# A decoder block on one core: low parts of one weight sum made by VectorE, output quarters of the down projection finished later, adaLN sums moved

## The chip, the cores and the metric

The kernel runs on one core of a Trainium2 chip. The metric is the device time of one execution in microseconds (us), the median of several. The engines are TensorE (PE, matmuls; PEld is its weight load), VectorE (DVE), ScalarE (ACT), GpSimd (POOL) and SyncE (SP, which here only issues DMAs). Each engine runs its own instructions in order and waits on semaphores for the others.

## The reference

One layer of a decoder block on x (512 tokens of 1024 channels, fp32), with a conditioning vector c. What matters here:

```python
mod = silu(c) @ ada_w + ada_b            # 6 x 1024: shift1, scale1, gate1, shift2, scale2, gate2
h   = rms_norm(x, norm1_g) * (1 + scale1) + shift1
...                                       # input projection, block-sparse attention, pooling, gates -> merged
x   = x + gate1 * (merged @ w_out)                       # "out"
h2  = rms_norm(x, norm2_g) * (1 + scale2) + shift2
u   = causal_dwconv3(h2 @ w_up) ; u_g, u_v = split(u)    # "up", 2 x 2816 channels
x   = x + gate2 * ((silu(u_g) * u_v) @ w_down)           # "down"
```

## The kernel before, in words

**Precision.** Each fp32 operand is split in two: a high part (a copy rounded to the type float32r) and a low part (the operand minus its high part). A product is three matmuls: high·high, low·high, high·low. They stand in helpers, so the profile names them by L133 to L135 and L139 to L141. The high copy is made by ACT (L114, L219), the low part by DVE (L124, L220).

**Products of blocks.** out, most of up, and down are computed as 2x2 blocks with seven products instead of eight. The seven are a11·b11, a12·b21, s1·t1, s2·t2, s4·b22, s3·t3, a22·t4: s are sums of blocks of the activations, t sums of blocks of the weights. In out, PE goes through them in that order (`o_prod`); in down the list `phases` (loop variable n, from 0) has the order a11·b11, s1·t1, s2·t2, a12·b21, s3·t3, s4·b22, a22·t4. The accumulators are PSUM banks called X, Y and Z, one for each of two row tiles p. A bank is copied or read between products (`o_keep`, `o_add`; `keep`, `finish`) and then accumulated further.

**Weights.** A unit is a tile of 128 x 1024. `load_unit` (L82) loads it on the SP queue to one of five buffers ("raw") that are used in rotation: a load waits until the tile five loads earlier has been read. Sums of weights (tsum for down, osum for out) are made in DRAM by accumulating DMAs on POOL's queue, long before they are used.

**out.** `o_split` loads a unit and has ACT make the two high parts and DVE the two low parts. The weight sum t3, fifth of the seven weight forms in the kernel's list FORMS, goes another way: `o_high` has ACT make the high parts and then negate the raw tile in place (L1043); POOL issues four DMAs that add the high parts to the negated tile (L1045); later `o_low` has ACT copy these, negated again, as the low parts (L1052). In ACT's order `o_low` stands behind the high parts of t4 and ahead of the squares of rows' tiles 0 and 1 (L1018), which the second RMS norm needs. That norm goes on with a sum on DVE (ms_y, L1022), a power on POOL (rs_y, L1024) and a scaling on DVE (xn, L1029). Behind s3·t3 and six matmuls of a22·t4, PE transposes the normalised tiles (`turn_h2(1)`, L907, tiles hT), then does the rest of a22·t4 and the first halves of up's units 0 and 1, then the second transposes (`turn_h2(3)`). `take_h2` turns them into h2 on ACT and DVE. POOL's queue in this stretch also holds the stores of x to DRAM (x2d, L1032) and fetches of x (L987).

**adaLN sums.** mod is 48 sums of 128 x 1024 on DVE (`ada_col(g, k)`: a load on SP and L207). Those of gate2, `ada_col(5, k)`, are spread: k = 0 in up's unit 3, k = 1 to 3 at the end of up, the rest in down.

**up.** Loop over 22 units j: matmuls on PE; two units behind them the convolution on ACT and DVE (`behind(0)`, L1127, L1131) and the gated product (`behind(1)`, L1146, L1153). Weights of unit j + 1 are prepared during unit j. The sums of down's weights run on POOL's queue at the same time.

**down.** For each of the seven products six units i; `unit` prepares the weights two units ahead. When a quarter of the output is complete, `finish` does three DVE steps of 128 x 512 (L1405 to L1413) and an output DMA on SP (L1414) for each of two row tiles.

The engines PE, DVE and ACT run in the order in which the code emits their instructions (`manual_schedule`); POOL and SP are ordered by the framework's scheduler.

Of the kernel before, what the change touches and what calls it, by code (L numbers as in the profile page):

```python
# [55 lines left out]
def block_kernel(tc, x, cvec, ada, wtok, wch, pool_w, wbr, wout, wup, wdn, pack, table, out):  # L56
# [4 lines left out]
    with ctx:  # L61
# [18 lines left out]
        def load_unit(src, name):  # L80
            raw = wraw_p.tile([P, src.shape[-1]], F32, tag="raw", name=f"raw_{name}")
            nc.sync.dma_start(raw, src)  # L82
            return raw
# [127 lines left out]
        def ada_col(g, k):  # L211
            ada_sum(g, k, ada_load(g, k))
# [820 lines left out]

        def o_high(nm):

            res = []
            for i in range(2):
                raw = load_unit(osrc(nm, i), f"wo_{nm}_{i}")
                for s in range(2):
                    hi = slot(f"wo_{nm}_{2 * i + s}_h", F32R)  # L1040
                    nc.scalar.activation(hi, raw[:, s * 512 : s * 512 + 512], AF.Copy)
                    res.append((hi, raw[:, s * 512 : s * 512 + 512]))
                nc.scalar.activation(raw, raw, AF.Copy, scale=-1.0)  # L1043
            for hi, r in res:
                nc.gpsimd.dma_start(r, hi.bitcast(F32), accum_op=ALU.add)  # L1045
            return res

        def o_low(nm, res):

            for k, (hi, r) in enumerate(res):  # L1050
                lo = slot(f"wo_{nm}_{k}_l", F32R)
                nc.scalar.activation(lo, r, AF.Copy, scale=-1.0)  # L1052
                wo[nm, k] = hi, lo

        o_prod("a11", "b11", "X", by_k=True)
# [23 lines left out]
        g_lo("s3")  # L1079
        t3 = o_high("t3")  # L1080
        for p in range(2):
# [4 lines left out]
        for i in range(2):  # L1086
            o_split("t4", i)
        o_low("t3", t3)
        o_prod("s4", "b22", "Y")
# [228 lines left out]
        for i in range(4):  # L1318
            ahead(f"up{i}", min(2, 2 * PLAIN - 1 - i))
            first.append((ready.pop(f"up{i}"), bank(f"u_{i}")))  # L1320
            up_mm(first[i][1], first[i][0], 0, 256)
            if i == 1:
                take_h2(3, turn_h2(3))
        for w, ps in first:
            up_mm(ps, w, 256, 512)
# [16 lines left out]
        for j in range(NP):  # L1342
# [18 lines left out]
            else:  # L1361
# [12 lines left out]
                if j in (2, 3):  # L1374
                    h_forms(j)
                if j == 3:
                    ada_col(5, 0)
            pend.append((j, *u))
# [4 lines left out]
        s_forms(NU - 2)  # L1383
        for k in range(1, 4):
            ada_col(5, k)
# [48 lines left out]
        def split_s(i):  # L1434
            forms["s2", i] = split_act(fa["s2", i], f"s2_{i}", width(i) // 2)

        for n, (an, bn, acc) in enumerate(phases):
            last = n == len(phases) - 1
            held_ = []
            for i in range(NU):  # L1440
                if n == 0 and i == 0:
                    ahead("b11_0", 3)
                w = unit(f"{bn}_{i}")
                a = forms.pop((an, i))
                if last and i >= NU - 2:
# [32 lines left out]
            if n == 0:  # L1478
                keep("s1", "X")
            elif n == 1:  # L1480
                keep("s5", "Y")
                g2 = row_of(5, "g2")
            elif n == 2:
                keep("s2", "X")
                fetch(0, 0)
            elif n == 3:
                for p in range(2):
                    finish(p, 0, 0, "Z", plus="s1")
                fetch(1, 1)
            elif n == 4:  # L1490
                for p in range(2):
                    finish(p, 1, 1, "X", minus=("s5", None))
                fetch(0, 1)
            elif n == 5:
                for p in range(2):
                    finish(p, 0, 1, "Y", minus=(None, "s2"))
                fetch(1, 0)
# [69 lines left out]
```

## Time and profile before

| | us |
|---|---|
| median of 3 runs | 668.15 |
| lowest, highest | 667.65, 668.96 |
| the profiled execution | 668.46 |
| its span in the trace | 666.7 |
| mean granted clock of PE | 0.992 |

Of one execution the profile has every instruction with start and duration, and what an idle engine waited for. A timeline row reads: start, duration, engine, line, operation, output<-input, size, xcount of merged instructions, and in brackets the idle time before it and who ended it. A windows row reads: stretch, length, then for PE, PEld, DVE, ACT and POOL the busy time with the number of instructions, then PE's granted clock, the DMA share and GB/s. Buffer numbers in names are left out there, so wo_t is any of the sums t1 to t4 of out. The end of a matmul is modelled, and neighbours overlap; the pace is seen in the starts.

### The profile page before, as it was taken

Reading aid. Unit: us, or ns where it says so; the run is one execution under the profiler, and the core shown is the slowest. Engines: PE = TensorE matmul, PEld = TensorE weight load, DVE = VectorE, ACT = ScalarE, POOL = GpSimd, SP = SyncE. Lnnn points to the kernel's source line nnn. Section 1 sums busy time; section 2 is a strip of 40 time slices with the busy share of each in tenths; the row PEclk is TensorE's granted clock in tenths of the full one; section 3 lists DMA queues with packets and bytes.
Section 4 is the critical chain, followed back from the end, with each engine's and each line's share of the span. In section 5 each row is a group of like instructions: output and inputs, shape, how many; then the busy total and the mean of one; then the engine's idle time right before and its main releaser. Section 6 shows DMA issues by size and latency. Waiting matters only on the chain.

```text
span 666.7 us, 9758 instructions
## 1 busy us (share of the span) xinstructions
PE 653.1 (98%) x3469; PEld 560.2 (84%) x3469; DVE 564.1 (85%) x966; ACT 392.3 (59%) x687; POOL 180.7 (27%) x243
## 2 busy tenths in 40 slices
PE   8999999999999999997999999999999999999997
PEld 6788788888888888875998899998999987888786
DVE  6997887898878868984869899998999799998775
ACT  8564346757655547583855575665756654758331
POOL 3004064432100055532544444444431000010000
PEclk9999999999999999996999999999999999999999
DMA  8887359999842785576489999999997235868761
GB/s 349 321 305 257 97 176 243 271 316 257 281 160 96 252 183 204 183 227 215 133 253 236 290 273 287 277 256 272 263 279 212 100 126 166 268 181 310 264 216 63
DMA packets 49031, 151.99 MB, mean 228 GB/s; under 512 B 6499, under 2 KB 7180, under 8 KB 48982
## 3 DMA queue, kind: packets, MB, share of 16 engines
q1 hardware_dynamic: 29510, 101.38, 44.7%
q0 software_dynamic: 19472, 49.98, 29.1%
q8 instruction: 27, 0.44, 0.3%
q14 instruction: 22, 0.18, 0.1%
HBM read 130.34 MB, written 19.95 MB: 225 GB/s over the span
## 4 chain that ended last, share of the span: by engine, by line
PE 81%; DVE 7%; DMA 5%; ACT 4%; issue 2%; POOL 1%; SPq 0%; ACTq 0%; DVEq 0%; POOLq 0%
PE u L134 6%; PE u L135 6%; PE u L133 6%; PE gate_ps L133 4%; PE gate_ps L135 4%; PE gate_ps L134 4%; PE uX L139 3%; PE uX L141 3%; PE uX L140 3%; DMA raw_wo_t<-wo_t_h 2%; PE q L149 2%; PE p L149 2%; PE X L140 2%; DMA raw_b<-in_wdn 2%; PE X L141 2%
## 5 line engine op out<-in xcount | busy, mean ns | idle before, releaser
L134 PE MATMUL u<-h2l,hi_up 128*128 128x512 f32 (+1 forms) x224 | 80.5, 360 | 0.1
L133 PE MATMUL u<-h2h,hi_up 128*128 128x512 f32 (+1 forms) x224 | 80.5, 359 | 0.0
L135 PE MATMUL u<-h2h,lo_up 128*128 128x512 f32 (+1 forms) x224 | 80.3, 359 | 0.0
L207 DVE CUSTOM_DVE_ANT_0 raw_ada<-raw_ada,cbc,pk 128x1024 f32<-128x1024 f32 x48 | 60.7, 1277 | 0.1
L133 PE MATMUL gate_ps<-h_h,hi_gate 128*128 128x512 f32 x128 | 50.1, 391 | 0.0
L135 PE MATMUL gate_ps<-h_h,lo_gate 128*128 128x512 f32 x128 | 50.0, 390 | 0.0
L134 PE MATMUL gate_ps<-h_l,hi_gate 128*128 128x512 f32 x128 | 49.9, 390 | 0.0
L134 PEld LDWEIGHTS u<-h2l,hi_up 128*128 128x128 f32 x224 | 42.3, 189 | 6.4 <-DVE h2l L923 0.3
L135 PEld LDWEIGHTS u<-h2h,lo_up 128*128 128x128 f32 x224 | 42.3, 189 | 6.2
L133 PEld LDWEIGHTS u<-h2h,hi_up 128*128 128x128 f32 x224 | 42.3, 189 | 6.1
L766 POOL DMA_DIRECT2D ta<-in_wdn x33 | 30.3, 917 | 19.1 <-DMA tsum_t<-ta 6.4
L841 POOL DMA_DIRECT2D g_d<-acol x2 | 1.8, 922 | 120.6 <-DVE acol L207 120.6
L767 POOL DMA_DIRECT2D tsum_t<-ta x33 | 18.6, 564 | 55.4 <-DMA ta<-in_wdn 52.2
L114 ACT ACTIVATE hi_t<-raw_t 128x1024 fp32r<-128x1024 f32 (+1 forms) x24 | 23.6, 985 | 16.8 <-PE X L141 7.1
L124 DVE TENSOR_TENSOR lo_t<-raw_t,hi_t 128x1024 fp32r<-128x1024 f32 (+1 forms) x24 | 26.6, 1129 | 4.2 <-ACT hi_t L114 4.2
L607 ACT ACTIVATE L<-L,mn 128x512 f32<-128x512 f32 (+3 forms) x32 | 17.6, 552 | 19.9 <-DVE mn L603 19.9
L135 PEld LDWEIGHTS gate_ps<-h_h,lo_gate 128*128 128x128 f32 x128 | 24.0, 188 | 5.1
L133 PEld LDWEIGHTS gate_ps<-h_h,hi_gate 128*128 128x128 f32 x128 | 24.0, 188 | 4.9 <-DVE mn L603 0.3
L134 PEld LDWEIGHTS gate_ps<-h_l,hi_gate 128*128 128x128 f32 x128 | 24.0, 188 | 4.5
L114 ACT ACTIVATE hi_up<-raw_up 128x1024 fp32r<-128x1024 f32 x24 | 24.9, 1049 | 4.3 <-PE u L134 4.3
L114 ACT ACTIVATE hi_b<-raw_b 128x1024 fp32r<-128x1024 f32 (+1 forms) x18 | 17.5, 983 | 16.3 <-PE X L141 4.9
L124 DVE TENSOR_TENSOR lo_b<-raw_b,hi_b 128x1024 fp32r<-128x1024 f32 (+1 forms) x18 | 19.9, 1129 | 6.0 <-ACT hi_b L114 6.0
(417 smaller groups left out, 2201.3 us busy)
## 6 DMA issues: line engine op xcount, KB each, us to landing
raw_ada<-in_ada SPq DMA_DIRECT2D x48, 512.0 KB, 5.5
raw_up<-in_wup SPq DMA_DIRECT2D x44, 512.0 KB, 6.5
ta<-in_wdn POOLq DMA_DIRECT2D x44, 256.0 KB, 6.4
raw_t<-tsum_t SPq DMA_DIRECT2D x20, 512.0 KB, 4.6
tsum_t<-ta POOLq DMA_DIRECT2D x33, 256.0 KB, 4.9
raw_gate<-in_wch SPq DMA_DIRECT2D x16, 512.0 KB, 4.4
raw_b<-in_wdn SPq DMA_DIRECT2D x15, 512.0 KB, 5.7
tc<-in_wdn POOLq DMA_DIRECT2D x22, 256.0 KB, 5.7
```

The lines of the kernel that those rows point to most:

```text
L114: nc.scalar.activation(hi, raw, AF.Copy)
L124: nc.vector.tensor_sub(lo, raw, hi.bitcast(F32))
L133: nc.tensor.matmul(ps, sh, mh, start=start, stop=False)
L134: nc.tensor.matmul(ps, sh, ml, start=False, stop=False)
L135: nc.tensor.matmul(ps, sl, mh, start=False, stop=stop)
L139: nc.tensor.matmul(ps, sh, mh, start=start, stop=False, skip_group_check=True)
L140: nc.tensor.matmul(ps, sh, ml, start=False, stop=False, skip_group_check=True)
L141: nc.tensor.matmul(ps, sl, mh, start=False, stop=stop, skip_group_check=True)
L149: nc.tensor.matmul(ps, sl if i else sh, mh if i else ml, start=False, stop=stop and i != late)
L207: nc.vector.tensor_tensor_reduce(out=raw, in0=raw, in1=cbc, op0=ALU.mult, op1=ALU.add, scale=1.0, scalar=col(C_AB + i), accum_out=acol[:, ...
L766: add = lambda to, nm: nc.gpsimd.dma_start(to, src(nm, i)[:, us], accum_op=ALU.add)
L767: store = lambda nm, t: nc.gpsimd.dma_start(dst[nm, i][:, us], t)
```

## The change

Three edits. (1) t3 of out goes through `o_split` like the others: its low parts are made by DVE, ahead of those of t4, and the functions `o_high` and `o_low` are gone. (2) `ada_col(5, 0)` and `ada_col(5, 1)` move from up's unit 3 and from the end of up to the place right behind the second transposes' `take_h2`. (3) In down, the `finish` of the three quarters that complete with n = 3, 4 and 5 is no longer done at the end of that product but, one row tile each, behind the weight preparation of units 0 and 1 of the next product.

```diff
-        def o_high(nm):
-            res = []
-            for i in range(2):
-                raw = load_unit(osrc(nm, i), f"wo_{nm}_{i}")
-                for s in range(2):
-                    hi = slot(f"wo_{nm}_{2 * i + s}_h", F32R)
-                    nc.scalar.activation(hi, raw[:, s * 512 : s * 512 + 512], AF.Copy)
-                    res.append((hi, raw[:, s * 512 : s * 512 + 512]))
-                nc.scalar.activation(raw, raw, AF.Copy, scale=-1.0)
-            for hi, r in res:
-                nc.gpsimd.dma_start(r, hi.bitcast(F32), accum_op=ALU.add)
-            return res
-        def o_low(nm, res):
-            for k, (hi, r) in enumerate(res):
-                lo = slot(f"wo_{nm}_{k}_l", F32R)
-                nc.scalar.activation(lo, r, AF.Copy, scale=-1.0)
-                wo[nm, k] = hi, lo
...
-        t3 = o_high("t3")
+        for i in range(2):
+            o_split("t3", i)
...
-        o_low("t3", t3)
...
                 take_h2(3, turn_h2(3))
+                ada_col(5, 0)
+                ada_col(5, 1)
...
-                if j == 3:
-                    ada_col(5, 0)
...
-        for k in range(1, 4):
+        for k in range(2, 4):
             ada_col(5, k)
...
+        due = []
...
                 w = unit(f"{bn}_{i}")
+                if due:
+                    due.pop(0)()
...
             elif n == 3:
-                for p in range(2):
-                    finish(p, 0, 0, "Z", plus="s1")
+                due = [lambda p=p: finish(p, 0, 0, "Z", plus="s1") for p in range(2)]
                 fetch(1, 1)
```

n == 4 and n == 5 are changed as n == 3 is.

ACT in out, before: from the copies of product s2·t2 (ok_s2) to the squares of tiles 0 and 1 (junk_y); _h and _l are high and low parts.

```order
L981 ACTIVATE ok_s2_0_3200<-oX_0_2961 128x512
L981 ACTIVATE ok_s2_1_3202<-oX_1_2965 128x512
L219 ACTIVATE wo_t4_0_h_3210<-raw_wo_t4_0_3208 128x512
L219 ACTIVATE wo_t4_1_h_3214<-raw_wo_t4_0_3208 128x512
L219 ACTIVATE wo_t4_2_h_3220<-raw_wo_t4_1_3218 128x512
L219 ACTIVATE wo_t4_3_h_3224<-raw_wo_t4_1_3218 128x512
L1052 ACTIVATE wo_t3_0_l_3228<-raw_wo_t3_0_3152 128x512
L1052 ACTIVATE wo_t3_1_l_3230<-raw_wo_t3_0_3152 128x512
L1052 ACTIVATE wo_t3_2_l_3232<-raw_wo_t3_1_3159 128x512
L1052 ACTIVATE wo_t3_3_l_3234<-raw_wo_t3_1_3159 128x512
L1018 ACTIVATE junk_y0_1_3264,ss_y0_3170<-x2_0_1_3124 128x512
L1018 ACTIVATE junk_y1_1_3270,ss_y1_3173<-x2_1_1_3126 128x512
```

The same place after:

```order
L981 ACTIVATE ok_s2_0_3202<-oX_0_2961 128x512
L981 ACTIVATE ok_s2_1_3204<-oX_1_2965 128x512
L219 ACTIVATE wo_t4_0_h_3212<-raw_wo_t4_0_3210 128x512
L219 ACTIVATE wo_t4_1_h_3216<-raw_wo_t4_0_3210 128x512
L219 ACTIVATE wo_t4_2_h_3222<-raw_wo_t4_1_3220 128x512
L219 ACTIVATE wo_t4_3_h_3226<-raw_wo_t4_1_3220 128x512
L1018 ACTIVATE junk_y0_1_3258,ss_y0_3172<-x2_0_1_3124 128x512
L1018 ACTIVATE junk_y1_1_3264,ss_y1_3175<-x2_1_1_3126 128x512
```

The four low parts of t3 have left ACT's order; they stand on DVE ahead of the four of t4.

DVE in down, before: the low parts of weight units (lo_t3_1 is unit 1 of t3) around the first `finish` (dt) and the last low parts of activations.

```order
L124 TENSOR_TENSOR lo_t3_1_6688<-raw_t3_1_6684,hi_t3_1_6686 128x1024
L220 TENSOR_TENSOR s4_5_l_6697<-s1_5_6178,s4_5_h_6696 128x256
L220 TENSOR_TENSOR a22_5_l_6701<-a22_5_6116,a22_5_h_6700 128x256
L1405 TENSOR_TENSOR dt_0_0_0_6704<-Z_0_6122,s1_0_6257 128x512
L1412 TENSOR_TENSOR dt_0_0_0_6704<-dt_0_0_0_6704,g2_0_6410 128x512
L1413 TENSOR_TENSOR dt_0_0_0_6704<-dt_0_0_0_6704,x2r_0_0_6550 128x512
L1405 TENSOR_TENSOR dt_1_0_0_6709<-Z_1_6123,s1_1_6259 128x512
L1412 TENSOR_TENSOR dt_1_0_0_6709<-dt_1_0_0_6709,g2_0_6410 128x512
L1413 TENSOR_TENSOR dt_1_0_0_6709<-dt_1_0_0_6709,x2r_1_0_6552 128x512
L124 TENSOR_TENSOR lo_t3_2_6722<-raw_t3_2_6718,hi_t3_2_6720 128x1024
L124 TENSOR_TENSOR lo_t3_3_6740<-raw_t3_3_6736,hi_t3_3_6738 128x1024
```

The same place after:

```order
L124 TENSOR_TENSOR lo_t3_2_6706<-raw_t3_2_6702,hi_t3_2_6704 128x1024
L1384 TENSOR_TENSOR dt_0_0_0_6708<-Z_0_6116,s1_0_6251 128x512
L1391 TENSOR_TENSOR dt_0_0_0_6708<-dt_0_0_0_6708,g2_0_6404 128x512
L1392 TENSOR_TENSOR dt_0_0_0_6708<-dt_0_0_0_6708,x2r_0_0_6544 128x512
L124 TENSOR_TENSOR lo_t3_3_6729<-raw_t3_3_6725,hi_t3_3_6727 128x1024
L1384 TENSOR_TENSOR dt_1_0_0_6731<-Z_1_6117,s1_1_6253 128x512
L1391 TENSOR_TENSOR dt_1_0_0_6731<-dt_1_0_0_6731,g2_0_6404 128x512
L1392 TENSOR_TENSOR dt_1_0_0_6731<-dt_1_0_0_6731,x2r_1_0_6546 128x512
L124 TENSOR_TENSOR lo_t3_4_6752<-raw_t3_4_6748,hi_t3_4_6750 128x1024
```

The low part of unit 2 now stands ahead of the three steps of row tile 0, and that of unit 3 ahead of those of row tile 1.

More of the change, by code (lines that the diff above doesn't have):

```diff
@@ L1486, in block_kernel @@
             elif n == 3:
-                for p in range(2):
-                    finish(p, 0, 0, "Z", plus="s1")
+                due = [lambda p=p: finish(p, 0, 0, "Z", plus="s1") for p in range(2)]
                 fetch(1, 1)
             elif n == 4:
-                for p in range(2):
-                    finish(p, 1, 1, "X", minus=("s5", None))
+                due = [lambda p=p: finish(p, 1, 1, "X", minus=("s5", None)) for p in range(2)]
                 fetch(0, 1)
             elif n == 5:
-                for p in range(2):
-                    finish(p, 0, 1, "Y", minus=(None, "s2"))
+                due = [lambda p=p: finish(p, 0, 1, "Y", minus=(None, "s2")) for p in range(2)]
                 fetch(1, 0)
```

## The prediction

> **What bounds the kernel now.** I read the page first, then the windows of equal length, the waits of TensorE (PE), and the timelines of PE, ScalarE (ACT), VectorE (DVE), GpSimd (POOL) and the SP queue around each place that the change touches.
>
> ```profile
> PE 653.1 (98%) x3469; PEld 560.2 (84%) x3469; DVE 564.1 (85%) x966; ACT 392.3 (59%) x687; POOL 180.7 (27%) x243
> ...
> PE oX L140 <- ACT wo_t_l L1052: 5.8, 4, 2.9
> ...
> PE X L140 <- DVE lo_t L124: 0.7, 1, 0.7
> PE X L140 <- DVE lo_b L124: 0.6, 1, 0.6
> ...
> PE uX L139 <- ACT ka L1294: 0.4, 1, 0.4
> ```
>
> PE is busy for 98% of the span, so an edit is worth what it takes out of PE's few gaps, or out of the slow-clock stretch behind a gap. Three waits (us in total, times, longest) belong to lines that the change touches: 5.8 us in out's product s3·t3, and 0.6 and 0.7 us in two products of down. The largest looks like this:
>
> ```profile
> 291.72 0.39 PE L139 MATMUL oY<-wo_b_h,gs_h 128*128 128x512 f32 x1
> ...
> 297.16 0.39 PE L139 MATMUL oX<-wo_t_h,gs_h 128*128 128x512 f32 x1
> ...
> 300.63 0.53 PE L140 MATMUL oX<-wo_t_l,gs_h 128*128 128x512 f32 x1 [1.94 <-ACT wo_t_l L1052]
> ...
> 304.89 0.79 PE L140 MATMUL oX<-wo_t_l,gs_h 128*128 128x512 f32 x1 [2.87 <-ACT wo_t_l L1052]
> ...
> 307.40 0.80 PE L140 MATMUL oX<-wo_t_l,gs_h 128*128 128x512 f32 x1 [0.86 <-ACT wo_t_l L1052]
> ...
> 313.83 1.92 PE L907 MATMUL hT<-pk,xn 128*128 128x128 f32 x16
> ```
>
> Between the first two rows stand the 24 matmuls of s4·b22: 5.44 us, 0.227 us each. From 297.16 to the first transpose at 313.83 there are 30 more (24 of s3·t3, 6 of a22·t4): 6.8 us at that pace, but 16.7 us passed. So 9.9 us are lost here, more than the 5.8 us of waits, because the clock fell too:
>
> ```profile
> 300.00:302.00 2.00, 1.37 (x3) 0.62 (x3) 1.93 (x4) 0.58 (x1) 0.58 (x1) 0.74 1.08 249
> ...
> 310.00:312.00 2.00, 2.00 (x7) 1.56 (x7) 0.21 (x1) 0.00 (x0) 0.00 (x0) 0.70 0.11 45
> ```
>
> The third number from the end is the granted clock. It fell within 300 to 302 and came back within 310 to 312, 3.9 us after the last gap's end if the return was at about 311.2 (0.70 is 1.2 us at 0.5 and 0.8 us at full).
>
> **Out: the low parts of t3.** Why PE waited, and who else did:
>
> ```profile
> 293.83 12.87 DMA raw_wo_t<-wo_t_h
> ...
> 306.72 0.63 ACT L1052 ACTIVATE wo_t_l<-raw_wo_t 128x512 fp32r<-128x512 f32 x1 [1.88 <-DMA raw_wo_t<-wo_t_h]
> ...
> 307.87 0.61 ACT L1018 ACTIVATE junk_y<-x 128x512 f32<-128x512 f32 x1
> ...
> 292.06 1.28 DVE L955 TENSOR_TENSOR gs_l<-gs,gs_h 128x512 fp32r<-128x512 f32 x2
> 295.68 2.50 DVE L220 TENSOR_TENSOR wo_t_l<-raw_wo_t,wo_t_h 128x512 fp32r<-128x512 f32 x4 [2.33 <-issue]
> 298.09 0.68 DVE L997 TENSOR_TENSOR ot<-oY,ok_s 128x512 f32<-128x512 f32 x1
> ...
> 301.59 0.69 DVE L1004 TENSOR_TENSOR x<-x,ot 128x512 f32<-128x512 f32 x1
> 308.61 0.21 DVE L1022 TENSOR_SCALAR ms_y<-ss_y 128x1 f32<-128x1 f32 x1 [0.40 <-ACT junk_y L1018]
> ...
> 313.27 0.87 DVE L1029 TENSOR_SCALAR xn<-x,rs_y 128x512 f32<-128x512 f32 x2
> ```
>
> The last accumulating DMA landed after 12.87 us, and ACT, which runs in order, stood at the t3 low parts until 307.3. Behind them were queued the squares of row tiles 0 and 1 (307.87), though their input was written by DVE at 302.3. So the normalisation, and the transposes at 313.83 that need its xn, were held by the same DMA.
>
> Removed: 4 accumulating DMAs on POOL's queue, 2 negations of 1024 columns and 4 low-part copies on ACT. Added: 4 DVE subtractions, 2.50/4 = 0.62 us each by the row at 295.68, which is the same operation. They start at 293.3, where DVE stood idle for 2.33 us, and end at 295.8, before PE wants them at 297.16. The four of t4 behind them then end at 298.3 instead of 298.2. If ACT makes t4's high parts no later than now (it has the two negations fewer ahead of it), the cost on DVE's path is about 0.15 us. PE runs s3·t3 from 297.16 to 302.6 without a gap.
>
> What is late next is the normalisation. The six steps of rows 0 and 1 on DVE end at 302.4 (now 302.3). ACT is free: its second square follows at 302.5, and DVE's ms of tile 1 comes 0.74 us after that square's start (307.87 to 308.61), at 303.25. Then POOL:
>
> ```profile
> 302.58 0.57 POOL L1032 DMA_DIRECT2D x2d<-x  x1 [1.47 <-DVE x L1004]
> 303.14 1.08 POOL L987 DMA_DIRECT2D x<-in_x  x2
> 308.30 1.17 POOL L1024 TENSOR_TENSOR rs_y<-ms_y,mhalf 128x1 f32<-128x1 f32 x2 [4.08 <-DVE ms_y L1022]
> ```
>
> POOL keeps its order: store of x, two fetches of x, then the two powers. With the store at 302.7, the powers start at 304.35 rather than at 303.4, and end at 304.95 and 305.5. DVE then does xn of tile 0 (0.87), one subtraction (0.6) and xn of tile 1, whose first half ends at about 306.95: the transposes flow from about **307.05** instead of 313.83. That is 6.8 us earlier. PE itself is there at 305.4: it waits until 304.05 to overwrite oX, which DVE's subtraction must read first (303.4 to 304.0), does six matmuls, then waits again. So a new pair of waits, some 1.45 and 1.6 us, takes the place of 9.9 us.
>
> Does all of the 6.8 us reach the end? The second set of transposes:
>
> ```profile
> 326.66 1.86 PE L907 MATMUL hT<-pk,xn 128*128 128x128 f32 x15 [0.40 <-DVE xn L1029]
> ```
>
> It follows the first by 12.83 us, and PE waits there for DVE even now. That chain (ACT's 16 steps on the transposed tiles, the DVE steps among them, squares, POOL's power, xn) starts from the first transposes, so it moves with them: 319.9. Behind that place PE's list of waits holds only the two of down and the 0.4 us of uX, so PE has no gap in which the time could be given back, and **6.8 us** stay gained.
>
> The clock is the open cost here. In the trace it fell once a gap of 1.94 us had ended; the new gaps are smaller, with six matmuls between. I take no fall. With a fall, 16 transposes take 1.9 us more, of which some 0.7 us are hidden by PE's present wait at 326.66 (0.40 and a little before the row): 1.3 us lost. [...]
>
> **Two adaLN sums earlier.** Sums (5,0) and (5,1) now stand behind the second set of transposed tiles; two SP loads move from behind up9 and b11_1 to behind up3.
>
> ```profile
> L207 DVE CUSTOM_DVE_ANT_0 raw_ada<-raw_ada,cbc,pk 128x1024 f32<-128x1024 f32 x48 | 60.7, 1277 | 0.1
> ...
> 338.17 1.23 DVE L124 TENSOR_TENSOR lo_up<-raw_up,hi_up 128x1024 fp32r<-128x1024 f32 x1 [3.12 <-ACT hi_up L114]
> ...
> 328.16 11.59 SPq L82 DMA_DIRECT2D raw_up<-in_wup  x3
> ...
> 345.38 2.00 ACT L114 ACTIVATE hi_up<-raw_up 128x1024 fp32r<-128x1024 f32 x2
> ...
> raw_up<-in_wup SPq DMA_DIRECT2D x44, 512.0 KB, 6.5
> ```
>
> Two sums are 2.5 us of DVE. DVE has 3.12 us of idle time at that place (335.05 to 338.17), so they cost nothing; without that cover the low parts of up4 would be 2.5 us later, still ahead of PE. Their loads wait for buffers of t3 and t4, free at 295.8 and 297.1 by the steps above. The price is in the ring of five load buffers: up7 now waits for the first sum (about 336.3 in today's times) instead of for up2's low part (328.2). With the median landing of 6.5 us it is there at 342.8, ahead of ACT's 345.4. Bounds: 0, and what the last rival says.
>
> At the end of up one sum of 1.2 us leaves DVE's path:
>
> ```profile
> 556.12 1.28 DVE L207 CUSTOM_DVE_ANT_0 raw_ada<-raw_ada,cbc,pk 128x1024 f32<-128x1024 f32 x1
> 557.33 0.74 DVE L1131 SCALAR_TENSOR_TENSOR ug<-u,pk,ug 128x511 f32<-128x511 f32 x1
> ...
> 561.09 3.50 DVE L124 TENSOR_TENSOR lo_b<-raw_b,hi_b 128x1024 fp32r<-128x1024 f32 x3 [0.19 <-ACT hi_b L114]
> ...
> 561.43 0.39 PE L139 MATMUL X<-hi_b,a_h 128*128 128x512 f32 x1
> 562.37 0.50 PE L140 MATMUL X<-lo_b,a_h 128*128 128x512 f32 x1 [0.55 <-DVE lo_b L124]
> ```
>
> PE's step took 0.94 us instead of 0.227: 0.71 us lost. The low part comes behind the convolutions, which came behind the sums; 1.0 to 1.2 us earlier covers it. Gain **0.7 us** (0 to 0.7).
>
> **Down: quarters finished later.** The six steps of the first finish now stand behind the low parts of t3's units 2 and 3 on DVE, and its output DMAs one and two loads further back on SP.
>
> ```profile
> 621.92 4.09 DVE L124 TENSOR_TENSOR lo_t<-raw_t,hi_t 128x1024 fp32r<-128x1024 f32 x4
> ...
> 622.14 0.39 PE L139 MATMUL X<-hi_t,s_h 128*128 128x512 f32 x1
> 623.19 0.50 PE L140 MATMUL X<-lo_t,s_h 128*128 128x512 f32 x1 [0.66 <-DVE lo_t L124]
> ```
>
> PE lost 1.05 − 0.23 = **0.8 us** to unit 2's low part, which waited for both finishes (6 × 0.68 us). It now comes 4.1 us earlier, and unit 3's, behind one finish, ends at about 622.2, ahead of PE's need after 624.8. A finish that is late costs nothing: Z and Y aren't written again, X only in a22·t4, a whole product later, and the output DMAs are far from the end. The other two quarters, behind the first units of s4·b22 and a22·t4, are moved where PE does not wait today: nothing.
>
> **The sum.** 6.8 + 0.7 + 0.8 = 8.3 us. The profiled execution took 668.46 us (span 666.7), 0.3 us above the median of 668.15; so 660.2 by its own time and **659.9** against the median. What a measurement here can tell from no change is about 0.2%, 1.3 us.
>
> **The rivals.** (1) The clock falls at the new gaps but is back when the transposes are through: 1.3 us dearer, 661.2. For it: the fall at 300.6. Against: no single gap is as long. Chance 0.22. (2) It falls and stays low through the transposes and for 3.9 us of matmuls behind them, as behind the last gap at 307.4: at half pace that is 1.9 us more, 663.1. No transpose here ran at a low clock, so the trace cannot say. [...] Chance 0.12. (3) The wait is replaced whole: the normalisation is held by something that I have not seen, and the transposes start near 313 as before. Then only 0.7 + 0.8 us are gained: 666.6. For it: POOL's power stands behind three DMA issues, and a late load of t4 would hold DVE at 298. Against: the row at 308.61 names ACT's square, and the square waited only for its place in ACT's order. Chance 0.08, with values between 664 and 666.6. (4) Slower: up7's load, issued 8 us later in a stretch that is full of transfers, comes so late that PE starves in up's unit 6. ACT is held once the landing takes over 345.4 − 336.3 = 9.1 us. PE takes that unit two units (48 matmuls, 10.9 us) after 344.8, at 355.7, and high and low parts need 4.4 us from 345.4, so PE feels a landing over 15 us, and the time is above 669.5 only over about 25 us: 670. The longest transfer in the rows above is 12.87 us. Chance 0.02.
>
> The forecast itself gets 0.52; 0.04 is left for what I have not thought of. The range 658.8 to 663.3 holds the forecast and rivals 1 and 2 (0.86, less some for the sizes): below, the waits that remain and 0.5 us of scatter; above, rival 2. Faster by over 0.2%: 0.94 (rival 3 counts in it down to about its upper end); within: 0.04; slower: 0.02.
>
> **What would show it.** After the change: no wait of PE on wo_t_l; the first transposes within 306.5 to 308; before them two PE waits, on DVE's subtraction and on xn, of under 2 us each; the squares of tiles 0 and 1 at about 300 and 302.5; granted clock 1.00 from 296 to 320 (else rival 1 or 2); the waits on lo_b and lo_t gone; no new wait between 340 and 365. Wrong would be a first transpose after 310, or a PE wait in the up stage.

## The result and the profile after

| | before | after |
|---|---|---|
| median (us) | 667.9 of 4 runs (666.27 to 668.96) | 660.09 of 4 runs (659.59 to 660.22) |
| the profiled execution | 668.46 | 660.07 |
| its span | 666.7 | 658.3 |
| mean granted clock of PE | 0.992 | 0.999 |

The ratio is 0.9884 (95% interval 0.9863 to 0.9905): faster by 7.8 us. Forecast were 659.9 us and a range of 658.8 to 663.3. The same kernel run again later, beside the experiments, gave 660.86 us beside 669.8 us for the kernel before, a ratio of 0.9867 (0.9846 to 0.9888).

These are the first row of the page of after, PE's entry in the slices of its clock, and the waits of PE that belong to changed places (us in total, times, longest):

```profile
PE 648.4 (98%) x3469; PEld 558.1 (85%) x3469; DVE 566.2 (86%) x970; ACT 388.8 (59%) x681; POOL 175.8 (27%) x239
...
PEclk9999999999999999999999999999999999999999
...
PE hT L907 <- DVE xn L1029: 1.4, 2, 1.0
...
PE oX L139 <- DVE ot L997: 1.1, 1, 1.1
```

The waits on wo_t_l, lo_b and lo_t are gone. PE's new waits are on DVE's subtraction (1.1 us) and on xn (1.0 us, and 0.4 that was there before). The clock has no slice below 0.9. PE's timeline at the place of the largest wait:

```profile
303.09 0.39 PE L141 MATMUL oX<-wo_t_h,gs_l 128*128 128x512 f32 x1
...
304.55 0.47 PE L139 MATMUL oX<-wo_t_h,mgh 128*128 128x512 f32 x1 [1.07 <-DVE ot L997]
...
306.03 0.27 PE L907 MATMUL hT<-pk,xn 128*128 128x128 f32 x1
307.31 1.86 PE L907 MATMUL hT<-pk,xn 128*128 128x128 f32 x15 [1.01 <-DVE xn L1029]
...
320.14 1.86 PE L907 MATMUL hT<-pk,xn 128*128 128x128 f32 x15 [0.40 <-DVE xn L1029]
```

s3·t3 runs through to 303.5; the transposes flow from 307.31 (before: 313.83), and the second set follows 12.83 us later, as it did before. To compare two executions, each place is measured from a landmark ahead of it, since executions here differ by up to 1.2 us ahead of any changed code:

| from, to (us) | before | after | difference |
|---|---|---|---|
| start to out's first matmul | 269.96 | 270.68 | +0.72 |
| s4·b22 to down's first matmul | 264.28 | 257.04 | −7.24 |
| down, a11·b11 (wait on lo_b) | 15.82 | 14.96 | −0.86 |
| down, s3·t3 (wait on lo_t) | 15.92 | 14.96 | −0.96 |
| span | 666.7 | 658.3 | −8.4 |

The first row holds no changed code. The next three are the places of the three edits: −9.1 together, and −8.3 with the start. Between the second transposes and down both executions take 229.34 us, to the hundredth: nothing is given back there. DVE's timeline of after in out, with the step that sets the new waits:

```profile
292.96 3.70 DVE L220 TENSOR_TENSOR wo_t_l<-raw_wo_t,wo_t_h 128x512 fp32r<-128x512 f32 x6
297.41 1.29 DVE L220 TENSOR_TENSOR wo_t_l<-raw_wo_t,wo_t_h 128x512 fp32r<-128x512 f32 x2 [0.75 <-ACT wo_t_h L219]
...
302.73 0.20 DVE L1022 TENSOR_SCALAR ms_y<-ss_y 128x1 f32<-128x1 f32 x1
303.60 0.21 DVE L1022 TENSOR_SCALAR ms_y<-ss_y 128x1 f32<-128x1 f32 x1 [0.67 <-ACT junk_y L1018]
303.73 0.68 DVE L997 TENSOR_TENSOR ot<-ok_s,oX 128x512 f32<-128x512 f32 x1
305.37 0.88 DVE L1029 TENSOR_SCALAR xn<-x,rs_y 128x512 f32<-128x512 f32 x2 [0.97 <-POOL rs_y L1024]
```

Four low parts of t3 and two of t4 run without a break, then DVE stands 0.75 us for the other two of t4. ACT's row tells why:

```profile
296.74 1.15 ACT L219 ACTIVATE wo_t_h<-raw_wo_t 128x512 fp32r<-128x512 f32 x2 [2.47 <-DMA raw_wo_t<-osum_t]
```

The load of t4's second unit is the last to land. It took 5.98 us from its issue at 290.74, against 4.00 us in before; why it took longer is not known. DVE sets its start too: the load waits for a buffer that DVE must read first, and is issued 0.03 us after that read ends.

```profile
289.49 1.22 DVE L124 TENSOR_TENSOR lo_up<-raw_up,hi_up 128x1024 fp32r<-128x1024 f32 x1
...
290.74 0.32 SPq L82 DMA_DIRECT2D raw_wo_t<-osum_t  x1
```

From 297.41 DVE runs to the first sum of squares; that sum (302.73) is the landmark for what follows it. POOL's timeline:

```profile
303.10 0.55 POOL L1032 DMA_DIRECT2D x2d<-x  x1 [1.50 <-DVE ms_y L1022]
303.65 1.07 POOL L987 DMA_DIRECT2D x<-in_x  x2
304.74 1.15 POOL L1024 TENSOR_TENSOR rs_y<-ms_y,mhalf 128x1 f32<-128x1 f32 x2
```

A store and two fetches (1.62 us) stand ahead of the powers, as the prediction had it, and DVE waits 0.97 us for the power. In down, DVE's timeline of after shows the finishes in their new places:

```profile
609.25 1.23 DVE L124 TENSOR_TENSOR lo_t<-raw_t,hi_t 128x1024 fp32r<-128x1024 f32 x1
610.39 0.68 DVE L1384 TENSOR_TENSOR dt<-Z,s 128x512 f32<-128x512 f32 x1
...
612.45 1.22 DVE L124 TENSOR_TENSOR lo_t<-raw_t,hi_t 128x1024 fp32r<-128x1024 f32 x1
613.58 0.68 DVE L1384 TENSOR_TENSOR dt<-Z,s 128x512 f32<-128x512 f32 x1
```

One low part stands ahead of each row tile's finish; PE's s3·t3 begins at 609.32 and meets no wait.

### The profile page after: what moved, and what is told of

The parts are those of the page before. It is cut to its first block, busy times and chain, and to the rows that moved or that the text cites. A ratio compares the mean times of both kernels' runs of the same rounds, so it can differ in the third digit from the quotient of the medians.

```text
span 658.3 us, 9756 instructions
## 1 busy us (share of the span) xinstructions
PE 648.4 (98%) x3469; PEld 558.1 (85%) x3469; DVE 566.2 (86%) x970; ACT 388.8 (59%) x681; POOL 175.8 (27%) x239
## 4 chain that ended last, share of the span: by engine, by line
PE 82%; DVE 8%; DMA 3%; issue 3%; ACT 2%; POOL 1%; SPq 0%; POOLq 0%; ACTq 0%; DVEq 0%
PE u L133 6%; PE u L134 6%; PE u L135 6%; PE gate_ps L133 4%; PE gate_ps L135 4%; PE gate_ps L134 4%; PE X L141 3%; PE X L140 3%; PE X L139 3%; PE uX L139 3%; PE uX L140 3%; PE uX L141 3%; DVE raw_ada L207 3%; PE O L644 2%; PE Y L140 2%
## 5 line engine op out<-in xcount | busy, mean ns | idle before, releaser
L841 POOL DMA_DIRECT2D g_d<-acol x2 | 1.8, 922 | 121.7 <-DVE acol L207 73.1
```

## The experiments

**Each edit alone.** Four kernels start from the kernel before and get one edit, or a part of one. Each ratio here and below is against the kernel before measured beside it, which took 669.6 to 669.9 us (median) in these measurements, not 667.9; so ratios are to be compared, not times.

Edit 1 (t3 through `o_split`):

```diff
...
-        t3 = o_high("t3")
+        for i in range(2):
+            o_split("t3", i)
...
-        o_low("t3", t3)
```

> The kernel before with the first edit alone (low parts of out's t3 by VectorE). Theory: the accumulating DMA held TensorE twice, at the low parts and, through ScalarE's order, at the normalisation. Then from the start of s4 x b22 in out to the second transposes 27.7 us pass, as with all three edits (34.9 us before), 7.2 us less, and the waits of 0.6 and 0.7 us in down on lo_b and lo_t stay as they were: about 660.8 us against 668. Rival, that a part of these 7.2 us comes from the earlier adaLN loads or from a freer SP queue: less than 6 us gained here, and over 28.5 us between the two places.

Measured: 664.23 us (661.78 to 665.59), ratio 0.9913 (0.9887 to 0.994). Its waits of PE:

```profile
PE oX L139 <- DVE ot L997: 2.7, 1, 2.7
...
PE X L140 <- DVE lo_t L124: 0.9, 1, 0.9
PE X L140 <- DVE lo_b L124: 0.6, 1, 0.6
```

The two waits of down stay, as expected of edit 1 alone: the terms are separate. But s4·b22 to the second transposes took 29.65 us, not 27.7, so 5.3 us were gained there, and PE's two new waits are one of 2.7 us. That is the sign that the rival gave (over 28.5 us, less than 6 us gained). Whether its cause holds too, that the other edits had a part in the gain, the kernels further on settle.

Edit 2 (two adaLN sums moved):

```diff
                 take_h2(3, turn_h2(3))
+                ada_col(5, 0)
+                ada_col(5, 1)
...
-                if j == 3:
-                    ada_col(5, 0)
...
-        for k in range(1, 4):
+        for k in range(2, 4):
```

> The kernel before with the second edit alone (two adaLN sums earlier). Theory: the one sum that leaves the end of up frees VectorE 1.2 us before b11's low parts, so the first product of down takes 15.0 us instead of 15.8 and TensorE's wait on lo_b is gone; nothing else moves, so the time is 0.8 to 0.9 us lower, 667.2 against 668. The wait on lo_t in s3 x t3 of down stays (about 0.8 us lost). Rival, that the two sums shorten VectorE's backlog through all of down: then the wait on lo_t goes too, and 1.7 us are gained. Rival on the other side: a new wait in up from the later load of up7, which would show as a wait of TensorE between 345 and 370 us and a time that is not lower.

Measured: 668.1 us (665.84 to 670.36), ratio 0.9981 (0.9965 to 0.9998). a11·b11 of down fell from 15.82 to 14.96 us: the wait on lo_b is gone. The one on lo_t grew:

```profile
PE X L140 <- DVE lo_t L124: 1.3, 1, 1.3
```

Edit 3 (finishes deferred):

```diff
+        due = []
...
+                if due:
+                    due.pop(0)()
...
-                for p in range(2):
-                    finish(p, 0, 0, "Z", plus="s1")
+                due = [lambda p=p: finish(p, 0, 0, "Z", plus="s1") for p in range(2)]
...
```

> The kernel before with the third edit alone (quarters of down finished behind the next product's first units). Theory: s3 x t3 of down takes 15.0 us instead of 15.9 and the wait on lo_t is gone, the wait on lo_b stays: 0.9 us lower, 667.1 against 668. Rival, that the wait on lo_t comes from VectorE's backlog of sums and not from the place of the finish: then it stays and the time is that of the kernel before.

Measured: 668.34 us (664.47 to 669.44), ratio 0.9976 (0.9956 to 0.9995). s3·t3 of down fell to 14.96 us, a11·b11 stayed at 15.83:

```profile
PE X L140 <- DVE lo_b L124: 0.6, 1, 0.6
```

By the ratios the three edits alone take off 0.87, 0.19 and 0.24%, 1.30% together; the whole change took off 1.16 and 1.33%.

Half of edit 2: only (5, 0) moves.

```diff
                 take_h2(3, turn_h2(3))
+                ada_col(5, 0)
...
-                if j == 3:
-                    ada_col(5, 0)
```

> The kernel before with half of the second edit: only sum (5,0) moves, from up's unit 3 to behind the second transposed tiles, and (5,1) stays at the end of up. Theory: TensorE has no wait in up that this could take away, so the first product of down still takes 15.8 us with the wait on lo_b, and the time is that of the kernel before within 0.3%. Rival, that a freer VectorE in up is what ends the wait: product one at 15.0 us.

Measured: 667.37 us, one run. a11·b11 took 15.84 us, so the wait on lo_b stays: it goes with (5, 1), the sum that leaves the end of up. But s3·t3 took 14.96 us: the wait on lo_t was gone, with no finish deferred. That nobody had expected, and it led to the next kernel.

**The wait on lo_t.** In the trace of before, the first row below is POOL issuing the store of the second gate (L841); the DMA view of the stretch 586 to 600 puts its landing 10.2 us later. Then ACT waits for a load of weights, b21's:

```profile
587.83 0.92 POOL L841 DMA_DIRECT2D g_d<-acol  x1 [75.15 <-DVE acol L207]
```
```profile
601.51 1.06 ACT L114 ACTIVATE hi_b<-raw_b 128x1024 fp32r<-128x1024 f32 x1 [4.79 <-DMA raw_b<-in_wdn]
```

The windows between (the last number is GB/s):

```profile
592.00:594.00 2.00, 2.00 (x10) 1.69 (x9) 2.00 (x4) 1.16 (x2) 0.00 (x0) 1.00 0.44 37
594.00:596.00 2.00, 2.00 (x10) 1.65 (x9) 2.00 (x4) 0.86 (x1) 0.00 (x0) 1.00 0.56 37
596.00:598.00 2.00, 2.00 (x11) 1.65 (x10) 2.00 (x4) 0.72 (x2) 0.00 (x0) 1.00 0.59 37
```

4 KB in 1024 pieces of 4 bytes go out, and all transfers together fall to 37 GB/s. From this store's issue to that high part it took 13.7 to 14.5 us in before, edit 1, edit 2 and edit 3 alone, but 11.2 us where only (5, 0) had moved (11.9 in after). The kernel that asks whether this store is the cause is the kernel before with the store written as 128 pieces of 32 bytes:

```diff
-            nc.gpsimd.dma_start(gd.rearrange("o (k p) -> p (o k)", p=P), acol[:, 8 * g : 8 * g + 8])
+            nc.gpsimd.dma_start(gd.rearrange("o (k p) -> p (o k)" if g == 2 else "o (p k) -> p (o k)", p=P), acol[:, 8 * g : 8 * g + 8])
```

> The kernel before, with one edit: the store g_d<-acol of the second gate, 1024 elements of 4 bytes to scattered places, is written as 128 rows of 32 bytes. The gate's elements then stand in another order, so the values of the last gating are not the reference's; the work is the same. In the kernel before, this store took 10.2 us, all transfers together fell to some 40 GB/s meanwhile, ScalarE waited 4.79 us for the load behind it, VectorE was late from there, and PE waited for lo_t in down's s3.t3. Theory: without the slow store the load lands early, the wait on lo_t is gone as in the kernel with one sum moved (s3.t3 of down 14.96 us instead of 15.92), though no finish has been deferred; the wait on lo_b stays; span 665.5 to 665.8. Rival: the wait on lo_t comes from the six steps of the finish alone, and stays at 0.5 us or more: span 666.4 or more, apart from scatter ahead of down.

Measured: 667.94 us (666.51 to 669.16), ratio 0.9974 (0.9961 to 0.9987), span 666.2. The store landed after 4.8 us, and ACT's row came 3.2 us earlier:

```profile
598.28 1.07 ACT L114 ACTIVATE hi_b<-raw_b 128x1024 fp32r<-128x1024 f32 x1 [1.14 <-PE X L141]
```

s3·t3 took 14.96 us, and PE's list has no wait on lo_t; a11·b11 stayed at 15.81 (lo_b). So that wait needs both: a load that lands late behind the small-element store, and the six finish steps ahead of the low part. With either one gone, it is gone. The span is 0.4 us above the expected one, all of it ahead of down: out took 0.4 us more here.

**What out's time follows.** In every kernel, DVE waits near 245 us for a unit of the branch stage's weights (3.03 us in after, 4.21 in before) and is late from then on. Its lateness is read as the start of the first gate sums (L938) less out's first matmul: 2.39 us in after, 3.90 in edit 1 alone. This kernel is after with 1.4 us more of DVE's work at that place:

```diff
                         nc.vector.tensor_sub(oc, R, gm[k + 4][:, 256:])
+                        nc.vector.tensor_sub(oc, R, gm[k + 4][:, 256:])
```

> All three edits, and VectorE writes the four quarters of out's first gate sum twice (the same values, 4 x 0.355 us = 1.4 us more for VectorE behind the branch stage, nothing else changed). Edit 1 alone left 29.65 us from the first matmul of s4.b22 to the second set of transposes, the whole change 27.70, while VectorE began those gate sums 3.90 and 2.39 us after out's first matmul. Theory: once edit 1 is made, out's time follows VectorE's lateness, so the shortfall of edit 1 alone was this lateness and not the other two edits: the stretch takes 29.1 us here (28.9 to 29.6), the span 659.6 to 660.0. Rival: it was the other two edits (the loads that they move), and VectorE's lateness is taken up by its idle time of 0.75 us ahead of t4's low parts and by the 1.27 us that the second square waits: the stretch stays under 28.2 us and the span under 658.9.

Measured: 662.75 us (662.04 to 663.24), ratio 0.9899 (0.9877 to 0.992). It began 3.21 us late; the stretch to the second transposes took 30.9 us, 3.2 us more than after. The theory's direction holds and the rival (under 28.2) falls, but the stretch and the span of 660.8 lie above the forecast. The trace shows why. The added steps cost 1.84 us, not 1.4: the four steps took 1.34 us in after (273.07 to 274.41), the eight took 3.18 here (273.15 to 276.33). So DVE was 2.66 us later than in after. DVE stood 0.2 us longer for t4 (0.95 against 0.75), and 0.4 us lies behind its first sum of squares (17.8 us to the second transposes, after 17.4), where the clock had fallen. Together that is 3.3 us for the 3.2 measured. The transposes, in after some 1.9 us, took

```profile
309.29 3.59 PE L907 MATMUL hT<-pk,xn 128*128 128x128 f32 x16
```

To ask for the clock alone, this kernel is after with xn of tile 0 written four times, to lengthen the gap ahead of the transposes:

```diff
             o_norm(p)
+            if p == 0:
+                for f in (0, 1) * 3:
+                    nc.vector.tensor_scalar(xn2[p, f], xr[p, f], rss[4 + p], None, op0=ALU.mult)
```

> All three edits, and VectorE writes the normalised tile 0 four times instead of once (6 x 0.40 = 2.4 us more between the first subtraction of s3.t3 and the second), so that TensorE's gap ahead of the first transposes grows from 1.0 to 3.4 us. Before the change the clock fell after a gap of 1.94 us. Theory (the first two rivals of the prediction, one or the other): it falls here too. If it is back when the transposes are through, the time is 1.3 us above the 2.4 us of the longer gap, a span of 662.0; if it stays low through the transposes and for 3.9 us of matmuls behind them, the 16 transposes take 3.7 us instead of 1.86 and the span is 663.9 to 664.1. The other view: it doesn't fall, the transposes keep 0.116 us each, the granted clock is 1.00 from 300 to 320, and the span is 660.7.

Measured: 663.47 us (662.06 to 664.68), ratio 0.9909 (0.9885 to 0.9934), span 662.9. DVE began 3.98 us late, like edit 1 alone (3.90); against that kernel the stretch from s4·b22 to down is 261.26 against 258.98 us, 2.28 more for 2.4 us of added steps. PE stood 2.49, 2.11 and 1.06 us before the transposes ran, and the clock fell only after the third of these. From DVE's first sum of squares to the second transposes it took 20.2 us, 17.8 without the added steps, so the fall cost 0.4 us against after. The theory had the fall right and its price wrong (1.3, or 3.2 and more), and it came later than either gap of over 2 us.

And the change itself, unaltered, once more:

> The change itself once more, unaltered, beside the next two. Its first run had VectorE early (the gate sums 2.39 us behind out's first matmul; in eight other kernels 2.75 to 4.03 us). Theory: the time of out follows that lateness, so with a usual value of 3.2 to 3.9 us the stretch from the first matmul of s4.b22 to the first of down takes 258 to 259 us, not 257.04, and the ratio to the kernel before is 0.989 to 0.991. Rival: the first run is typical, the stretch stays at 257.0 to 257.3 whatever the lateness, and the ratio is 0.988 or less.

Measured: 660.86 us (659.59 to 662.72), ratio 0.9867 (0.9846 to 0.9888), span 659.1. DVE began 3.57 us late, and s4·b22 to down took 258.43 us, not 257.04: the theory's 258 to 259. Its ratio of 0.989 to 0.991 was a miss, since the ratio lies below that. PE's waits again became one:

```profile
PE oX L139 <- DVE ot L997: 2.1, 1, 2.1
```

and in this execution the clock did fall. The kernels so far in one table (us; the spell is the stretch at half clock between 294 and 322, read in windows of 0.1 us):

| kernel | DVE late by | s4·b22 to down | half-clock spell |
|---|---|---|---|
| before | 3.43 | 264.28 | 10.2 |
| edit 2 alone | 4.03 | 265.82 | 13.7 |
| edit 3 alone | 3.04 | 264.22 | 10.3 |
| half of edit 2 | 2.75 | 263.68 | 6.8 |
| before, store in larger pieces | 2.49 | 264.65 | 6.8 |
| after | 2.39 | 257.04 | none |
| after again | 3.57 | 258.43 | 3.4 |
| edit 1 alone | 3.90 | 258.98 | 3.4 |
| after, DVE 1.4 later | 3.21 + 1.84 | 260.27 | 6.8 |
| after, xn written four times | 3.98 | 261.26 | 3.4 |

From "after" on stand the kernels with edit 1. In those above, the stretch does not follow the lateness (264.65 us at 2.49, 264.22 at 3.04): there the accumulating DMAs ahead of t3's low parts (12.87 us to the last landing in before) set it. With edit 1 it does: from s4·b22 to DVE's first sum of squares, after took 10.29 us, and after again, edit 1 alone and xn written four times took 1.03, 1.60 and 1.42 us more, for 1.18, 1.51 and 1.59 us of added lateness. DVE's idle time ahead of t4 does not take this up, since the load that it waits for is issued behind DVE's own read. At a lateness of some 3.5 us, before took 264.28 and after again 258.43; edit 1 alone differs from after again by 0.55 us with 0.33 of lateness. So the 1.95 us that edit 1 alone fell short were lateness (1.51 us) and the fallen clock (some 0.36 us, below), a matter of the execution and not of edits 2 and 3: the rival's cause does not hold.

**Can the new waits be shortened?** Four more orders of the same work, all with the three edits. First, the two fetches behind the powers on POOL:

```diff
-        o_fetch(1, 0)
         o_prod("s3", "t3", "X")
...
         o_prod("a22", "t4", "X", (0,), range(2))
+        o_fetch(1, 0)
+        for p in range(2):
+            for f in range(2):
+                o_store(p, f)
```

> All three edits, and the two fetches of x for row tiles 2 and 3 are issued by GpSimd behind the two powers, not ahead of them. In the change the two fetches took 1.07 us between the last store and the first power, and VectorE then waited 0.97 us for the power ahead of the normalised tile. Theory: the powers come 1.0 us earlier, VectorE goes from its subtraction straight to the normalised tile, and the first transposes flow 0.9 to 1.0 us earlier, the second set too: span 657.3 to 657.5. Rival: the powers are not what it waits for (the second square, or VectorE's own order, ends last), or x, fetched 2 us later, is what the residual of tiles 2 and 3 then waits for: span 658.3 or more.

Measured: 660.3 us (659.34 to 661.38), ratio 0.9863 (0.9841 to 0.9886), span 657.6, with a lateness of 3.21. From DVE's first sum of squares to the second transposes it took 16.36 us, after 17.41: the 1.05 us less that the theory had; the span is 0.1 us above its figure, with DVE 0.8 us later than in after. Then DVE's order as well:

```diff
...
+        o_root(0)
+        tail = [o_add(2, 1, "X", minus=("s5", None))]
+        o_root(1)
+        for f in range(2):
+            for p in range(2):
+                o_xn(p, f)
+        tail.append(o_add(3, 1, "X", minus=("s5", None)))
...
```

> As the kernel with the fetches behind the powers, and VectorE's order in out is changed: the first subtraction of s3.t3 ahead of the second tile's sum of squares, the second subtraction behind the four normalised tiles (its bank is only written again behind the transposes), and those in the order in which the transposes want them (first halves of both tiles, then second halves). Theory: TensorE starts the six matmuls of a22.t4 at 303.6 instead of 304.55 and ends them at 305.1, the first two normalised halves are there at 305.2, and the transposes start without a wait worth speaking of, 2.0 to 2.1 us earlier than in the change: second set at 318.1, span 656.2. Rival: the transposes start earlier, but the chain behind them is bound by VectorE, which has the second subtraction and four residual steps still before it: the second set gains 0.8 to 1.2 us and the span is 657.1 to 657.5.

Measured: 659.65 us (657.77 to 661.2), ratio 0.9852 (0.9824 to 0.988), span 657.9. The same path took 16.00 us, 1.41 less than after: between the theory (2.0 to 2.1) and the rival (0.8 to 1.2). PE goes straight from its six matmuls to the transposes; what is late next is the chain behind them, as the rival said. In this kernel's timeline DVE has no idle time from its first xn to the sum of squares of tile 2:

```profile
305.30 1.83 DVE L1028 TENSOR_SCALAR xn<-x,rs_y 128x512 f32<-128x512 f32 x4 [0.48 <-POOL rs_y L1024]
...
316.86 0.21 DVE L1022 TENSOR_SCALAR ms_y<-ss_y 128x1 f32<-128x1 f32 x1
```

So one of DVE's two squares in this stretch went to ACT:

```diff
-        take_h2(1, tps, {3: first_half, 5: lambda: o_square(2, 1, True), 6: lambda: o_square(3, 1, True)})
+        take_h2(1, tps, {3: first_half, 5: lambda: o_square(2, 1, True)})
...
             o_square(2 + p, 0)
+            if p == 0:
+                o_square(3, 1)
             o_root(2 + p)
```

> As the kernel with VectorE's order changed, and one of the two squares that VectorE makes between the two sets of transposes (row tile 3, second half; 0.95 us with its read-out) goes to ScalarE, which stood idle for 1.98 us behind its first square there. In the kernel before it VectorE was busy without a break from the first normalised tile to the last sum of squares but one, so its steps set the second set of transposes. Theory: the last sum of squares comes 0.9 to 1.0 us earlier, the second set too, until TensorE itself is the bound (its waits there were 0.33 and 0.40 us and a hole of 0.3 us): 16.0 us from VectorE's first sum of squares to the second set become 15.1 to 15.3, and the stretch from s4.b22 to down gets 0.7 to 0.9 us shorter at equal lateness of VectorE: 255.8 to 256.0 if it begins 3.44 us late. Rival: ScalarE is the bound with the third square, and nothing or less than 0.3 us is gained.

Measured: 659.02 us (657.84 to 660.51), ratio 0.9841 (0.9824 to 0.9859), span 657.0. The path took 15.39 us: 0.6 us gained, a little under the theory's 0.7 to 0.9, and more than the rival's 0.3 (stretch to down 256.37 us, at a lateness of 3.67). This kernel has the lowest median of the study. Beside it in the same comparison the change itself had 0.9867; the intervals overlap, so the traces show the gain (2.0 us on that path) more clearly than the times. Last, the cause of DVE's lateness, by asking for out's weights one iteration later in the branch stage:

```diff
-            o_split(("b11", "b21", "t1", "t2")[j // 2], j % 2, nc.gpsimd)
+            if j:
+                o_split(("b11", "b21", "t1", "t2")[(j - 1) // 2], (j - 1) % 2, nc.gpsimd)
...
+        o_split("t2", 1, nc.gpsimd)
```

> As the last kernel, and each load of out's weights in the branch stage is asked for one iteration later, so that the branch stage's third load stands ahead of the first of them in the queue, not behind it. In all runs so far VectorE waited 1.6 to 4.8 us for the high part of that unit near 245 us and was late from then on. Theory: that wait shrinks to under 1 us, VectorE begins the gate sums 2.0 to 2.4 us behind out's first matmul (TensorE's branch products are the floor), and out gets shorter by what the lateness falls: stretch of 254.6 to 255.2 us from s4.b22 to down. Rival: the wait moves to the next unit, whose load is now the late one, and the lateness stays at 3 to 4 us.

Measured: 659.53 us (659.02 to 661.3), ratio 0.9853 (0.9836 to 0.987), span 657.6. The wait shrank to 0.97 us and DVE began the gate sums 1.70 us late, as the theory had it and better; but the stretch to down took 256.82 us, nothing gained. DVE lost it again at once, as its timeline shows:

```profile
273.07 1.78 DVE L867 TENSOR_TENSOR mgl<-gate,mgh 128x512 fp32r<-128x512 f32 x1
274.78 2.52 DVE L942 TENSOR_TENSOR gs<-gs,gate 128x256 f32<-128x256 f32 x4
```

These two groups take 0.68 and 1.42 us in the kernel without this edit. Each lost 1.1 us, the second in the first of its four steps (1.51 us instead of 0.41), while POOL did the low parts that the edit had pushed to this place:

```profile
272.99 3.01 POOL L220 TENSOR_TENSOR wo_t_l<-raw_wo_t,wo_t_h 128x512 fp32r<-128x512 f32 x2 [1.82 <-ACT wo_t_h L219]
```

Then t4's last load cost another 1.13 us, and by the first sum of squares DVE was later than without the edit. Neither view had this.

## Why the prediction was right, point by point

**Out.** The step held: ACT's low parts and the DMA ahead of them were the wait, s3·t3 runs through, and the chain to the second transposes moves as a whole (12.83 us before and after). Forecast was 6.8 us. The first execution gained 7.24, of which 1.04 came from DVE being early by chance (2.39 against 3.43); at like lateness (before 3.43, after again 3.57) the runs show 5.85. So the step is worth some 6.0 to 6.2 us (5.85 and the 0.14 us of lateness between those two; 7.24 less 1.04). One condition of the forecast failed. It had t4's low parts right behind those of t3, if t4's high parts came no later than before. At like lateness those of its second unit did come later: 5.33 us behind the start of s4·b22 in after again, 4.29 in before; DVE stood 0.60 us for them there, 0.75 in after, 0.86 in edit 1 alone. This late load (some 0.5 us) and the fallen clock (0.36, below) are the 0.8 us between 6.8 and 6.0. That the first total came as close as it did is in part luck: DVE's early start gave back more than the late load took. The power on POOL, priced at 1.62 us of issues, was there, as the kernel with the fetches behind it shows by 1.05 us.

**The new waits.** Forecast as 1.45 and 1.6 us; measured 1.07 and 1.01 in one execution, 2.1 and none in the other. Both are set by DVE, as said.

**The clock.** The forecast's case (no fall) is what the first execution did, and rival 1 is what the second did: the same kernel does either. Its price was wrong. From DVE's first sum of squares to the second transposes, after took 17.41 us without a fall, after again 17.78 and edit 1 alone 17.76 with one: 0.36 us, not 1.3. Judged by the mean clock of each run (0.997 in the trace with the fall, 0.999 in the one without), it fell in two of this kernel's nine runs. At half clock the six matmuls fill the time in which PE waited for xn: in after again that wait has left PE's list ahead of the first transposes. What hides the slow transposes was not tried by itself.

**Rival 2** had the clock stay low through the transposes and for a further 3.9 us, an estimate from the stretch behind the gap at 307.4. That does not hold here. In the kernel with DVE 1.4 us later, PE's windows, with its busy time behind the length and the clock third from the end, are:

```profile
302.49:305.90 3.41, 0.25 (x2) 1.00 0.79 310
305.90:309.32 3.42, 2.72 (x7) 0.50 0.70 230
309.32:312.73 3.41, 3.41 (x18) 0.50 0.08 31
312.73:316.14 3.41, 3.41 (x16) 1.00 0.32 123
```

The third stretch holds 16 transposes and two matmuls, the transposes 3.3 of its 3.41 us, and at its end the clock was back.

**Two sums earlier.** Forecast 0.7 us, measured 0.86. The step was sized by one matmul's delay; the whole product is 0.86 us longer. The last rival (up7's load late) did not come: up, from the second transposes to down, takes 229.34 us in both.

**Down.** Forecast 0.8 us, measured 0.96. The mechanism was half of it: the finish steps did push the low part, but only because a load had been late behind the small-element store. In half of edit 2 and with the store in larger pieces the wait was gone with the finishes where they were. In after again the load was as late as in before (13.8 us from store to high part, before 13.7) and there was no wait, so the deferred finishes are enough. The sum is right for this kernel as it stands; with the store in larger pieces PE had no wait on lo_t left for this edit to remove.

**The sum.** 8.3 us forecast. The spans of the first two profiles differ by 8.4, with DVE early by 1.0 and a start 0.7 later. The second profile (659.1) lies 7.6 below the same 666.7, but that is from another measurement; side by side the medians differ by 7.8 us in the first measurement and 8.9 in the second, whose interval of 7.5 to 10.3 holds the forecast. At like lateness the places of the three edits give 6.0 to 6.2, 0.86 and 0.96 us: 7.8 to 8.0.

## What to carry to other kernels

Where an engine that runs in order stands for a slow DMA, price what is queued behind it as well: here the wait named was 5.8 us, but in before the last xn started at 313.27 and the transposes at 313.83, so the step was worth 6 only because the normalisation behind that DMA moved with it. Once that wait was gone, DVE's start set the time (1.03 to 1.60 us for 1.18 to 1.59 us of added lateness), and with it the issue of a load (0.03 us behind DVE's own read): compare executions from a landmark close to the change, at equal lateness of that engine. A wait that needs two causes is removed by either, as that on lo_t was (14.96 us with either gone), so an edit's gain can vanish when another one is made.

## What the runs showed of the hardware

**The granted clock changed in steps of 3.41 us.** Spells at half clock lasted 3.4, 6.8, 10.2 and 13.7 us: one to four times 3.41. In before it fell at 300.96, was back at 311.20 and fell again at 666.18, behind the last matmul: 10.24 us, then 354.98, and 104 times a third of 10.24 is 354.99. Below, PE's windows are cut from such a change in steps of that length. In after again:

```profile
301.91:305.32 3.41, 1.31 (x7) 1.00 0.67 263
305.32:308.73 3.41, 3.41 (x12) 0.50 0.52 154
308.73:312.15 3.42, 3.42 (x22) 1.00 0.20 78
```

and in the kernel with the lengthened gap:

```profile
302.17:305.58 3.41, 1.71 (x8) 1.00 0.82 326
305.58:309.00 3.42, 1.63 (x6) 1.00 0.71 198
309.00:312.41 3.41, 1.23 (x9) 1.00 0.08 32
312.41:315.82 3.41, 3.41 (x14) 0.50 0.20 77
```

A window with 1.31 or 1.23 us of work was followed by half clock, one with 1.71 or 1.63 was not. So here 2.49 us of gap that fell across two windows cost no clock, and 2.1 us inside one did; a gap of 1.94 us in before did (1.30 us of work from 297.55 to 300.96), one of 1.97 us in the kernel with the later fetches did not. In edit 2 alone a window with 1.65 us of work was followed by a fall; the busy times of a trace, whose matmul ends are modelled, do not tell it from the 1.63 that was not. The same cut through all fourteen traces has 15 falls, those at the kernels' ends included: each came after a window with 0.16 to 1.65 us of work, and no window at full clock that was not followed by a fall had under 1.63. The way back was not the same: in before two windows, with 1.06 and 2.03 us of work, were followed by half clock, and full clock came behind the third, a full one.

```profile
304.37:307.79 3.42, 2.03 (x4) 0.50 1.02 399
307.79:311.20 3.41, 3.41 (x9) 0.50 0.70 264
311.20:314.61 3.41, 3.41 (x20) 1.00 0.00 0
```

The most work in a window at half clock that was followed by half clock was 2.72 of 3.42 us, in the kernel with DVE 1.4 us later; all nine returns came behind a full window.

**A 4 KB store held up the loads.** In 1024 pieces of 4 bytes it took 10.2 us and all transfers together fell to 37 GB/s; in 128 pieces of 32 bytes it took 4.8 us, the mean of the same stretch, 586 to 600, went from 152 to 281 GB/s, and the high part behind the load came 3.2 us earlier.

**Two DVE steps took longer beside POOL.** One DVE step of 0.68 us took 1.78, and one of 0.41 took 1.51, when they started 0.08 and 0.51 us into a subtraction on POOL. A product that reads a PSUM bank (gate<-gate,A) kept its 0.69 us at 264.89 in the same trace, wholly beside another such subtraction.
